# A two-layer decoder trunk on one core: token statistics moved behind their tile's matmuls, and two changes of PSUM bank

## The chip, the cores and the metric

The kernel runs on one core of one Trainium2 chip. The time is device time in microseconds (us) of one execution; the median of three executions is given. The profiled execution is one more, taken by the hardware profiler, with its own time and span. The engines are called as in the profile: PE (TensorE matmul), PEld (its weight load), DVE (VectorE), ACT (ScalarE), POOL (GpSimd), SP (SyncE, which issues the DMAs). "Granted clock" is the share of the full TensorE clock that was granted.

## The reference

All tensors are float32; 512 tokens, 1024 channels, two residual layers. Layer 0 has the gated and the attention mixer, layer 1 the matrix memory; each is followed by an MLP.

```python
def reference(x, ...):
    for layer in range(2):
        h = _rmsnorm(x, mix_norm_g[layer])
        x = x + (_even_mixer(h, ...) if layer % 2 == 0 else _odd_mixer(h, ...))
        h = _rmsnorm(x, mlp_norm_g[layer])
        x = x + jnp.square(jax.nn.relu(h @ mlp_w1[layer])) @ mlp_w2[layer]
    return x

def _rmsnorm(x, g):
    return x * lax.rsqrt(jnp.mean(x * x, -1, keepdims=True) + 1e-6) * g

def _even_mixer(h, ...):
    p = h @ w_in                                  # 1024 -> 2560
    za, zb = jax.nn.gelu(p[..., :1024]), p[..., 1024:]
    u, vg = za[..., :512], layernorm(za[..., 512:])   # groups of 64 columns
    y_a = u * (causal 128x128 mixing of vg per group + bias)
    q, k, v = zb in three parts; q and k RMS-normed per head of 64
    y_b = stick_breaking(q, k, v)                 # strictly causal attention, 8 heads
    return concat([y_a, y_b]) @ w_out

def _odd_mixer(h, ...):
    p = h @ w_in                                  # q, k, v, output gate, 8 gate columns
    hc = mlstm(silu(conv(q, k)), v, gates)        # 4 heads, chunks of 128
    return (rmsnorm(hc) * sigmoid(og)) @ w_out
```

## The kernel before

**Precision.** Every matrix product is made of three matmuls. An operand a is split into a high part (ACT copies it to the matmul type) and a low part (DVE subtracts the high part): a `hi`/`lo` pair. `mm3` (L289 to L292) issues high x high, high x low and low x high. Weights are read from HBM in units of 128 x 1024 (`w_load`), split by `w_split` (L189 on ACT, L190 on DVE, for a few units on POOL) and taken in order by `w_take`, which also starts the splitting of the next units. Raw units have two buffers there, split ones five.

**Norms.** The RMS norm is taken apart: the matmuls use x times the channel gain g, and the factor of the token, (mean square + eps)^-1/2, is applied to the product afterwards. For the first projection x comes in four tiles of 128 tokens. `x_load` brings a tile (or a half of it) in by DMA, multiplies it by g (L358, tile `xg`) and splits it into `xhi` and `xlo` (L286, L287). `x_stats` squares the tile on ACT (L363, `xq`, two buffers), adds the eight channel blocks on POOL in three steps (L365), and calls `norm_cols`: a matmul with a column of 1/1024 (L266, in a PSUM bank "C"), the addition of eps on DVE (L268), and a power on POOL (L270), which gives `r1[t]`; L368 keeps eps times the mean square in `er2[t]`. In the text `x_stats(0)` stands between the loads of tiles 2 and 3, the other three behind the last load, all of them ahead of the first chunk.

**The first projection.** `act_chunk` runs a chunk of 512 output columns over the four token tiles: 24 matmuls to a tile (8 channel blocks x 3) into one PSUM bank, then an evacuation. The chunks are vg, u, k, q and v. `vg_evac` (L407) applies Gelu with the factor `r1[t]` on ACT, then the layer norm of the row on DVE with a power on POOL (L415), and splits the result. The banks are called A (two), B (three), C (two) and O (one); the first chunks take A, A, O in turn.

**The MLP.** The hidden units are computed in four groups; the second product of a group is a 2 x 2 block product made of seven block products (`PROD`) instead of eight, in `second` (L658 to L714), each of 24 matmuls of 256 columns for each of two column halves s. `accm` collects what several groups share; in the last group (`done`) it is added to the residual `xs` and the finished rows are handed on (`yield d`) or shipped to HBM (`ship`). Before, product n1 is added to block (1, 1) of the residual from its bank "c", then n4 is accumulated on top of n1 in the same bank, and their sum is added to block (1, 0) in two halves (L709 to L714).

**Between blocks.** `enter` (L331 to L343) follows a generator that finishes the residual row by row: it scales and splits each row for the next layer (L282, L283), squares it (L335, L338) and adds up the squares (L339, on POOL, the last on DVE), and ends with `norm_cols`. `w_out` (L321 to L328) is an output projection: eight rows of channels, each in a PSUM bank named by `tags`, added to the residual by DVE (L327).

**Order.** Each engine works through its own queue in order. Which instruction stands where is settled before the run by a planner that lays the instructions out by simulated times, with earlier text ahead of later text among what is ready; semaphores follow from the tiles that are read and written. `tc.issue_after(ins)` makes the instructions traced in its block that run on the engine of `ins` stand behind `ins`.

## Time and profile before

| | |
|---|---|
| three executions | 1136.91, 1133.94, 1134.82 us, median 1134.82 |
| profiled execution | 1136.92 us, span 1135.1 us, granted clock 0.994 |
| PE busy | 1106.8 us, 98% of the span |
| PEld busy | 960.1 us, 85% |
| DVE busy | 828.4 us, 73% |
| ACT busy | 524.3 us, 46% |
| POOL busy | 161.9 us, 14% |
| DMA | 105.18 MB, mean 93 GB/s |

The span is the part of the execution in which the profiler saw the engines work. Busy time is the time in which an engine had at least one instruction running; matmuls overlap, so their durations add up to more. In rows of the profile "out<-in" are the tiles by the program's names; "[1.23 <-POOL xq L365]" behind a row says that the engine sat idle for 1.23 us before it and that POOL's instruction of line 365 on tile xq ended that.

### The profile page before, as it was taken

The numbers are of one execution on the slowest core, as the hardware profiler recorded it, in microseconds if no ns is written. First come the engines' busy times: TensorE is split into PE (matmuls) and PEld (weight loads), VectorE is DVE, ScalarE is ACT, GpSimd is POOL, SyncE is SP. The second block draws the span as 40 slices with busy tenths as digits, with TensorE's granted clock in tenths as the row PEclk, the third lists the DMA queues.
The fourth block names the chain that finished last, engine by engine and source line by source line (L and its number), as shares of the span: only waits on it lengthen the run. The fifth ranks groups of instructions, "written<-read, shape, count | busy, mean of one in ns | idle before, by whom it ended". The sixth has DMA issues, their size and how long they took to land.

```text
span 1135.1 us, 15928 instructions
## 1 busy us (share of the span) xinstructions
PE 1106.8 (98%) x6372; PEld 960.1 (85%) x6372; DVE 828.4 (73%) x1151; ACT 524.3 (46%) x800; POOL 161.9 (14%) x154
## 2 busy tenths in 40 slices
PE   8999979999999999999999999999999999999998
PEld 5788767878988988988988888887899899899898
DVE  7753599469957957957977676679887677677676
ACT  5343677445435435435555444435443444444442
POOL 7216554550000000000130010003100000000000
PEclk8999999999999999999999999999999999999999
DMA  6322310242241241341042203304324224224121
GB/s 230 93 75 79 104 41 1 74 168 93 94 132 72 96 138 65 100 143 56 20 132 76 94 19 112 94 31 155 112 74 141 82 74 147 76 75 149 38 84 66
DMA packets 34506, 105.18 MB, mean 93 GB/s; under 512 B 3712, under 2 KB 10112, under 8 KB 34432
## 3 DMA queue, kind: packets, MB, share of 16 engines
q1 hardware_dynamic: 34432, 104.17, 28.3%
q8 instruction: 50, 0.82, 0.3%
q14 instruction: 24, 0.20, 0.1%
HBM read 102.06 MB, written 2.10 MB: 92 GB/s over the span
## 4 chain that ended last, share of the span: by engine, by line
PE 82%; DVE 10%; POOL 3%; ACT 2%; issue 2%; DMA 1%; SPq 0%; DVEq 0%; ACTq 0%; POOLq 0%
PE psA L292 10%; PE psA L290 10%; PE psA L291 10%; PE psB L674 7%; PE psB L676 7%; PE psB L675 7%; PE psC L292 5%; PE psC L291 5%; PE psC L290 5%; DVE m L537 2%; PE psO L290 2%; PE psO L291 2%; PE psO L292 2%; DVE wl L190 2%; DMA wr<-wall 1%
## 5 line engine op out<-in xcount | busy, mean ns | idle before, releaser
L189 ACT ACTIVATE wh<-wr 128x1024 fp32r<-128x1024 f32 (+1 forms) x124 | 131.2, 1061 | 170.1 <-DMA wr<-wall 53.0
L190 DVE TENSOR_TENSOR wl<-wr,wh 128x1024 fp32r<-128x1024 f32 (+1 forms) x108 | 135.9, 1265 | 81.7 <-ACT wh L189 49.9
L189 ACT ACTIVATE wh<-wq_s 128x1024 fp32r<-128x1024 f32 x64 | 67.0, 1060 | 127.4 <-PE psC L291 56.3
L291 PE MATMUL psA<-xlo,wh 128*128 128x512 f32 x292 | 115.3, 395 | 0.0
L292 PE MATMUL psA<-xhi,wl 128*128 128x512 f32 x288 | 114.2, 396 | 0.5 <-DVE wl L190 0.5
L290 PE MATMUL psA<-xhi,wh 128*128 128x512 f32 x288 | 112.5, 392 | 1.1 <-DVE xres L327 1.1
L292 PE MATMUL psC<-xhi,wl 128*128 128x512 f32 x256 | 101.5, 396 | 0.0
L291 PE MATMUL psC<-xlo,wh 128*128 128x512 f32 x256 | 101.3, 396 | 0.0
L290 PE MATMUL psC<-xhi,wh 128*128 128x512 f32 x256 | 100.4, 392 | 0.0
L292 PE MATMUL psA<-wh,xlo 128*128 128x512 f32 (+2 forms) x232 | 88.1, 381 | 2.1 <-DVE xlo L287 1.8
L290 PE MATMUL psA<-wh,xhi 128*128 128x512 f32 (+2 forms) x232 | 88.7, 385 | 1.2 <-ACT wh L189 1.0
L291 PE MATMUL psA<-wl,xhi 128*128 128x512 f32 (+2 forms) x232 | 88.3, 382 | 1.1 <-DVE wl L190 1.1
L189 ACT ACTIVATE wh<-wq 128x1024 fp32r<-128x1024 f32 x48 | 50.8, 1058 | 79.0 <-PE psB L675 30.2
L339 POOL TENSOR_TENSOR ssq<-ssq,sq 128x512 f32<-128x512 f32 x18 | 31.6, 1753 | 346.7 <-ACT sq L338 346.7
L190 DVE TENSOR_TENSOR wl<-wq_s,wh 128x1024 fp32r<-128x1024 f32 x64 | 77.6, 1220 | 2.5 <-ACT wh L189 2.5
L290 PEld LDWEIGHTS psA<-xhi,wh 128*128 128x128 f32 x288 | 54.7, 190 | 13.8 <-ACT sq L338 1.5
L686 DVE TENSOR_TENSOR xres<-xres,psB 128x512 f32<-128x512 f32 (+1 forms) x96 | 54.7, 592 | 15.2 <-PE psB L676 15.1
L733 DVE SCALAR_TENSOR_TENSOR r<-psC,rrow 128x512 f32<-128x512 f32 x32 | 22.1, 690 | 59.6 <-PE psC L292 59.6
L291 PEld LDWEIGHTS psA<-xlo,wh 128*128 128x128 f32 x292 | 54.9, 188 | 12.3
L292 PEld LDWEIGHTS psA<-xhi,wl 128*128 128x128 f32 x288 | 54.1, 188 | 12.2 <-DVE wl L190 0.8
L190 DVE TENSOR_TENSOR wl<-wq,wh 128x1024 fp32r<-128x1024 f32 x48 | 58.6, 1221 | 2.2 <-ACT wh L189 2.2
L290 PEld LDWEIGHTS psC<-xhi,wh 128*128 128x128 f32 x256 | 48.6, 190 | 10.9
(396 smaller groups left out, 3146.6 us busy)
## 6 DMA issues: line engine op xcount, KB each, us to landing
wr<-wall SPq DMA_DIRECT2D x122, 512.0 KB, 3.5
wq<-wall SPq DMA_DIRECT2D x64, 512.0 KB, 3.6
out<-xres SPq DMA_DIRECT2D x16, 128.0 KB, 1.8
wr<-wv SPq DMA_DIRECT2D x2, 528.0 KB, 3.6
xres<-xT SPq DMA_DIRECT2D x4, 256.0 KB, 6.2
xres<-xT SPq DMA_DIRECT2D x2, 512.0 KB, 8.9
lngb<-lngb SPq DMA_DIRECT2D x1, 512.0 KB, 5.6
sgr<-sgw SPq DMA_DIRECT2D x1, 512.0 KB, 6.3
```

What stands on the lines that cost most here:

```text
L189: act.activation(hi[:, :n], raw, AF.Copy)
L190: (gp if i in POOL_LO else dve).tensor_tensor(lo[:, :n], raw, f(hi[:, :n]), op=ALU.subtract)
L290: pe.matmul(out, lhsT=lh, rhs=rh, start=first, stop=False)
L291: pe.matmul(out, lhsT=lh, rhs=rl, start=False, stop=False)
L292: pe.matmul(out, lhsT=ll, rhs=rh, start=False, stop=last)
L339: (dve if i == KT - 1 else gp).tensor_tensor(ssq, ssq, j, op=ALU.add)
L537: dve.tensor_tensor_scan(m[:, ::-1], m[:, ::-1], ones.to_broadcast([P, n]), 1.0, op0=ALU.mult, op1=ALU.mult)
L674: pe.matmul(o, lhsT=lh, rhs=rh, start=first, stop=False, skip_group_check=True)
L675: pe.matmul(o, lhsT=lh, rhs=rl, start=False, stop=False, skip_group_check=True)
L676: pe.matmul(o, lhsT=ll, rhs=rh, start=False, stop=fin, skip_group_check=True)
L686: add = lambda dst, b, op=ALU.add: dve.tensor_tensor(dst, dst, b, op=op)
L733: dve.scalar_tensor_tensor(r, b, 0.0, rb[0], op0=ALU.max, op1=ALU.mult)
```

## The change

Three edits. (1) `x_stats` is cut in two: `x_square` makes the squares and the adds, `x_stats` the matmul, eps, power and `er2`. `act_chunk` gets an argument `behind`, and calls it after the last matmul of each token tile, with the matmuls that it issues placed behind that one on TensorE; the vg chunk passes `x_stats`. The multiplication by g of tiles 1 to 3 is done by DVE instead of POOL, and the square of tile 0 is called before the loads of the other tiles. (2) In the last group of a layer n1's bank is closed with n1 alone; n1 is added to block (1, 1) and to block (1, 0), and n4 begins anew in a bank of the tag "C". (3) The odd layer's last output projection takes its banks in the order A, A, B, B instead of A, A, O.

```diff
@@ mm3
-        pe.matmul(out, lhsT=ll, rhs=rh, start=False, stop=last)
+        return pe.matmul(out, lhsT=ll, rhs=rh, start=False, stop=last)
@@ act_chunk
-    def act_chunk(hus, per, width, evac, tags=tags):
+    def act_chunk(hus, per, width, evac, tags=tags, behind=None):
...
-                mm3(b[:, :width], xhi[:, kt, tts(t)], xlo[:, kt, tts(t)], hi[:, o:o + width], lo[:, o:o + width],
-                    kt == 0, kt == KT - 1)
+                i = mm3(b[:, :width], xhi[:, kt, tts(t)], xlo[:, kt, tts(t)], hi[:, o:o + width], lo[:, o:o + width],
+                        kt == 0, kt == KT - 1)
+            if behind:
+                with tc.issue_after(i.ins):
+                    behind(t)
             evac(t, b[:, :width])
@@ first projection
-        def x_stats(t):
-            q = ld.tile([P, KT, P], F32, name=f"xq{t}", tag="xq", bufs=2)
+        xq = [None] * NT
+
+        def x_square(t):
+            q = xq[t] = ld.tile([P, KT, P], F32, name=f"xq{t}", tag="xq", bufs=2)
             act.activation(q, xs[:, :, tts(t)], AF.Square)
             for k in (4, 2, 1):
                 gp.tensor_tensor(q[:, :k], q[:, :k], q[:, k:2 * k], op=ALU.add)
-            me, r1[t] = norm_cols([q[:, 0, :]])
+
+        def x_stats(t):
+            me, r1[t] = norm_cols([xq[t][:, 0, :]])
             e = sm(1, "er2")
             dve.tensor_scalar(e, me, EPS, None, op0=ALU.mult)
             er2[t] = e
...
-        x_load(1, 0, 4, gp)
-        x_load(1, 4, 8, gp)
-        x_load(2, 0, 8, gp)
-        x_stats(0)
-        x_load(3, 0, 8, gp)
+        x_square(0)
+        x_load(1, 0, 4, dve)
+        x_load(1, 4, 8, dve)
+        x_load(2, 0, 8, dve)
+        x_load(3, 0, 8, dve)
         for t in range(1, NT):
-            x_stats(t)
+            x_square(t)
...
-        act_chunk(w_take(4), 2, 512, vg_evac)
+        act_chunk(w_take(4), 2, 512, vg_evac, behind=x_stats)
@@ mlp, second
-                    add(blk(1, 1, s), prod("n1", "c", True, False))
+                    b = prod("n1", "c", True, done)
+                    add(blk(1, 1, s), b)
                     ship(1, 1, s)
-                    b = prod("n4", "c", False, True)
+                    if done:
+                        add(blk(1, 0, s), b)
+                    b = prod("n4", "e" if done else "c", done, True, "C")
@@ odd layer
-        r = enter(w_out(w_take(2), y_of(3), "AAO"), 3, ssq)
+        r = enter(w_out(w_take(2), y_of(3), "AABB"), 3, ssq)
```

## The prediction

> **What bounds the kernel now.** I read the page first (shares of the engines), then the waits of TensorE, then the busy time by stretch, then the order of time at the four places that the diff touches. Times are us from the start of the span.

> ```profile
> PE 1106.8 (98%) x6372; PEld 960.1 (85%) x6372; DVE 828.4 (73%) x1151; ACT 524.3 (46%) x800; POOL 161.9 (14%) x154
> ```

> ```profile
> ...
> PE psB L674 <- DVE xres L686: 2.6, 2, 1.6
> ...
> PE psC L266 <- POOL xq L365: 2.1, 2, 1.2
> ```

> TensorE is the bound, 98% of the span. So time can come only out of its idle 28.3 (1135.1 - 1106.8) and out of matmuls that ran at a lower clock. The waits (columns: total, times, longest) name two causes that the diff touches; two single waits of the kind stand in the rows of parts 1 and 3.

> ```profile
> 0.00:46.00 46.00, 38.83 (x141) 28.00 (x142) 36.39 (x48) 22.82 (x27) 28.68 (x30) 0.89 0.55 179
> 8.00:34.00 26.00, 21.17 (x80) 16.53 (x81) 23.81 (x22) 12.88 (x15) 23.44 (x16) 0.86 0.60 195
> 100.00:250.00 150.00, 138.63 (x700) 110.75 (x699) 103.83 (x143) 89.14 (x171) 80.44 (x59) 0.99 0.21 64
> 562.00:585.00 23.00, 21.11 (x172) 20.50 (x170) 22.23 (x26) 12.91 (x18) 12.15 (x14) 1.00 0.39 115
> 780.00:802.00 22.00, 20.68 (x88) 15.63 (x86) 21.96 (x24) 13.70 (x20) 9.86 (x7) 1.00 0.57 191
> ```

> Columns: the stretch, its length, busy time of PE, PEld, DVE, ACT and POOL, granted clock, DMA share, GB/s. The first 46 us lose most: 7.2 idle and a clock of 0.89. Between 8 and 34 both DVE (23.81 of 26) and POOL (23.44) are nearly full. At 562 to 585 and 780 to 802 DVE has hardly a gap either: whatever TensorE saves there may be taken back by a vector operation that comes no earlier.

> **Part 1, the first projection.** The change takes the four gating multiplies from POOL to DVE, and the mean-square matmuls from where the planner had put them to just behind the 24 products of their token tile. Squares, adds, matmuls and powers stay in number, and the DMAs keep their order on SP's queue.

> ```profile
> 8.93 0.50 PE L291 MATMUL psA<-wl,xhi 128*128 128x512 f32 x1 [1.06 <-DVE wl L190]
> ...
> 10.33 0.63 PE L292 MATMUL psA<-wh,xlo 128*128 128x512 f32 x1
> 10.75 0.63 PE L290 MATMUL psA<-wh,xhi 128*128 128x512 f32 x1
> 12.61 0.59 PE L266 MATMUL psC<-onesd,xq 128*128 128x1 f32 x2 [1.23 <-POOL xq L365]
> 13.06 0.77 PE L291 MATMUL psA<-wl,xhi 128*128 128x512 f32 x1
> ...
> 29.14 0.40 PE L291 MATMUL psO<-wl,xhi 128*128 128x512 f32 x1
> 29.37 0.39 PE L292 MATMUL psO<-wh,xlo 128*128 128x512 f32 x1
> 29.61 0.28 PE L266 MATMUL psC<-onesd,xq 128*128 128x1 f32 x2
> 30.72 0.38 PE L266 MATMUL psC<-onesd,xq 128*128 128x1 f32 x2 [0.84 <-POOL xq L365]
> 30.96 0.48 PE L290 MATMUL psA<-wh,xhi 128*128 128x512 f32 x1
> 31.28 0.40 PE L291 MATMUL psA<-wl,xhi 128*128 128x512 f32 x1
> ...
> 33.51 0.79 PE L292 MATMUL psA<-wh,xlo 128*128 128x512 f32 x1 [1.83 <-DVE xlo L287]
> ...
> 36.97 0.40 PE L291 MATMUL psA<-wl,xhi 128*128 128x512 f32 x1
> ```

> That was TensorE's order of time (start, duration, line, operation, what ended the idle time before). DVE's, and then its groups between 8 and 34 (count, busy time, mean ns, idle before):

> ```profile
> 3.99 0.69 DVE L358 TENSOR_TENSOR xg<-xres,par 128x512 f32<-128x512 f32 x1 [2.28 <-DMA xres<-xT]
> ...
> 10.49 3.14 DVE L190 TENSOR_TENSOR wl<-wr,wh 128x1024 fp32r<-128x1024 f32 x2
> ```

> ```profile
> L190 DVE TENSOR_TENSOR wl<-wr,wh 128x1024 fp32r<-128x1024 f32 x5 | 9.1, 1830 | 0.0
> L287 DVE TENSOR_TENSOR xlo<-xg,xhi 128x512 fp32r<-128x512 f32 x3 | 3.5, 1180 | 1.6 <-ACT xhi L286 1.6
> L287 DVE TENSOR_TENSOR xlo<-xg,xhi 128x1024 fp32r<-128x1024 f32 x2 | 3.5, 1769 | 0.0
> ```

> The same weight split between 300 and 500, and POOL's groups of the first 50 us:

> ```profile
> L190 DVE TENSOR_TENSOR wl<-wr,wh 128x1024 fp32r<-128x1024 f32 x22 | 26.6, 1221 | 16.6 <-PE psB L676 15.8 <-ACT wh L189 0.8
> ```

> ```profile
> L365 POOL TENSOR_TENSOR xq<-xq 128x512 f32<-128x512 f32 (+2 forms) x12 | 13.6, 1143 | 7.6 <-ACT xq L363 7.3
> L358 POOL TENSOR_TENSOR xg<-xres,par 128x512 f32<-128x512 f32 (+1 forms) x4 | 8.4, 2088 | 0.0
> L270 POOL TENSOR_TENSOR rc<-me,nhalf 128x1 f32<-128x1 f32 x4 | 3.5, 890 | 4.9 <-DVE me L268 4.9
> ```

> A product at full speed takes 0.23 from start to start (29.14 to 29.37). Four terms:

> (a) Tile 0. The product of 13.06 stood behind the statistics, which waited for POOL's adds. It needs the first of the two weight splits that began at 10.49 and took 3.14 together, so that one ended near 12.06. TensorE can resume at 12.1: 0.95 gained.

> (b) The statistics of tiles 1 and 2 kept the products from 29.61 to 30.96, and the next start came 0.32 later instead of 0.23: 1.44 in all. A pair alone costs 0.24 (30.72 to 30.96) and that 0.09, so 0.33, and three pairs now stand between the tiles, 1.0 (tile 0's was counted in (a), tile 3's was paid before too). Gain 0.45.

> (c) Tile 3 waited for its low part from 31.51 (31.28 + 0.23) to 33.51: 2.0. The multiply ahead of that split was POOL's last. POOL loses 8.4; DVE gains two multiplies of 0.69 and two of twice the size, taken at twice that, 4.1. Is the low part then in time? From 12.06 DVE owes two weight splits (3.7), the multiplies (4.1) and four splits of x (2 x 1.18 + 2 x 1.77 = 5.9), at the crowded prices of now: 25.8. Tile 3 wants it near 30. Even 4 us of other work put ahead would not delay it.

> (d) After that wait eight starts, 33.51 to 36.97, took 3.46 instead of 8 x 0.23 = 1.84: 1.6 lost at the lower clock, gone with the wait. Here idling for about 2 us was enough to lower it. [...] The trace shows the loss, so I count it.

> Part 1: 0.95 + 0.45 + 2.0 + 1.6 = 5.0. The norm factor now comes about 1.5 after its tile (pair, DVE, a power of 0.89 on POOL), and the evacuation on ACT waits for it; behind it wait the next weight splits on ACT, not yet wanted, and its PSUM bank, wanted two tiles of 24 x 0.23 = 5.5 later. POOL's adds are 12 x 1.14 / 4 = 3.4 a tile. The squares have two buffers, so tile 2's waits for tile 0's pair, near 18 (tile 2 ended at 29.6, two tiles earlier is 18.5, less (a)); square and adds end near 23, wanted near 29. The next weight units are released by TensorE's own progress and move with it.

> **Part 2, the last product of a layer.** In the last group n4 gets a bank of its own, and n1 is added to two blocks instead of being summed with n4 first.

> ```profile
> 1127.02 1.29 DVE L686 TENSOR_TENSOR xres<-xres,psB 128x512 f32<-128x512 f32 x2 [3.89 <-PE psB L676]
> ...
> 1127.17 0.28 PE L676 MATMUL psB<-n1h,wl 128*128 128x256 f32 x1
> ...
> 1128.45 0.36 PE L674 MATMUL psB<-n4h,wh 128*128 128x256 f32 x1 [1.00 <-DVE xres L686]
> ```

> ```profile
> 572.89 0.28 PE L292 MATMUL psO<-wh,xlo 128*128 128x264 f32 x1
> 574.80 0.39 PE L674 MATMUL psB<-n4h,wh 128*128 128x256 f32 x1 [1.63 <-DVE xres L686]
> ...
> 584.39 0.51 PE L292 MATMUL psA<-wh,xlo 128*128 128x264 f32 x2 [0.26 <-DVE xlo L283]
> ```

> These matmuls start 0.12 apart (half the columns of 0.23). At the end of the kernel n4 could start at 1127.29 instead of 1128.45: 1.15. The added DVE add (0.65, half of 1.29) ends near 1129.0, n4 near 1130.2, so it is covered, and only the final adds and the output follow, which move along. In the first layer the same wait is worth up to 574.80 - 573.01 = 1.8, but there DVE is busy 22.23 of 23, gets two adds more (1.3), and already ends the stage: TensorE waits for low parts of x at 584.39. Bounds -1.3 and 1.8; nearest to a full DVE, I take 0.3.

> **Part 3, banks AABB** for the odd layer's last output projection: the following MLP's first bank no longer waits for the last adds.

> ```profile
> 788.68 0.39 PE L292 MATMUL psA<-yoh,wl 128*128 128x512 f32 x1
> 790.18 0.47 PE L290 MATMUL psA<-xhi,wh 128*128 128x512 f32 x1 [1.11 <-DVE xres L327]
> ...
> 795.09 2.44 DVE L283 SCALAR_TENSOR_TENSOR xlo<-xres,par,xhi 128x512 fp32r<-128x512 f32 x2
> ```

> TensorE could go on at 788.91 instead of 790.18: 1.3. But the last low parts come at 797.5 from a DVE busy 21.96 of 22, and without them the first MLP product cannot end. Bounds 0 and 1.3; I take 0.5.

> **Sum:** 5.0 + 1.15 + 0.3 + 0.5 = 6.95. The profiled execution took 1136.92 (its span and 1.8 around it), so 1130.0 for it. It lay 2.1 above the median of the three runs, 1134.82, from which I forecast **1127.9**. The three lie 3.0 apart, so some 0.3%, 3.4 us, is what can be told from no change.

> **Rivals.**

> *The clock recovers in tile 0.* If the shorter pause before the product of 13.06 (0.9 instead of 1.9) lets the clock rise at once, some eight starts take 0.23 instead of 0.42 (10.33 to 10.75): 1.5 more, 1126.4. Against it: the pause of 1.06 before 8.93 was followed by starts at the lower clock. [...] Chance 0.12.

> *DVE becomes the bound of the start.* It gets 4.1 more where 2.2 are free. For it: a weight split takes 1.83 beside a busy POOL and 1.22 later. Against it: POOL's work falls by 8.4 of 23.4. If masks, gate weights and evacuations are put ahead, tile 3 still waits and tile 1 waits by another 1 us: of part 1 only (a) and (b) less 1 are left, 0.4, with the rest 2.35: 1132.5. [...] Chance 0.17.

> *The norm factor comes late.* If the power for tile 0 is queued on POOL behind the adds of tiles 2 and 3, it ends near 30, and the bank that tile 3 wants near 29.6 is free near 30.8: 1.2 idle and 1.6 of clock, 1130.7. Chance 0.05.

> *The planner lays out attention otherwise.* The order on the engines follows simulated times, which shift. TensorE idles 11.4 between 100 and 250 (150 - 138.6); half as much again is 5.7: 1133.6. Chance 0.08.

> *Slower: TensorE stalls behind each tile.* The pairs stand in order in its queue, so where a tile's adds are late, the next tile's products wait too. [...] It decides from adds that end over 6 us later than I reckon. Chance 0.08.

> **How the numbers follow.** The forecast has 0.50, with a range of its own from 1125.6 (upper bounds of parts 2 and 3) to 1130.0 (lower ones). The range of all, 1123.8 to 1133.0, adds both of the clock's gain below and the DVE case above; it leaves out the slow case, most of attention's and a tail of either side, 0.18. Faster than 1131.4: 0.50 + 0.12 + 0.05, and a quarter of the DVE case, 0.71. Slower than 1138.2: 0.08. Same: 0.21.

> **What would show it.** Right: in the first 40 us no wait of L292 for xlo and none of L266 for xq; each L266 pair behind 24 products; a clock above 0.93 over the first 46; POOL without L358; n4 in psC at the end, 0.12 behind n1. Near 573 and 790 the waits gone, but a new one of about 1 us for xlo L283 near 583 and 796. Wrong: TensorE waiting in tile 1 or 3 for xlo, L266 waiting for L365 behind a tile, L407 late enough that a product waits for its bank, or an idle sum between 100 and 250 far from 11.4.

## The result, and the profile after

The change made the kernel slower: 1141.92 us (median of six, 1140.51 to 1143.23) against 1135.59 (six, 1133.56 to 1137.73), ratio 1.0056 [1.0045, 1.0066]. The forecast was 1127.9. The profiled execution took 1140.83, span 1139.1, 4.0 more than before.

First the page's line of TensorE, then its list of waits (total, times, longest), both of the changed kernel.

```profile
PE 1108.0 (97%) x6372; PEld 962.1 (84%) x6372; DVE 831.1 (73%) x1159; ACT 522.9 (46%) x800; POOL 155.2 (14%) x150
```

```profile
PE psC L266 <- DVE ssq L343: 5.3, 2, 3.9
...
PE psA L290 <- ACT sq L342: 2.5, 1, 2.5
PE psA L290 <- ACT xhi L282: 2.2, 1, 2.2
...
PE psA L292 <- DVE xlo L283: 1.5, 1, 1.5
...
PE psA L291 <- DVE xlo L283: 1.1, 1, 1.1
```

The two kinds of wait named in the prediction, n4 for the residual and L266 for xq, are gone. New ones stand in their place, at the end of the first layer and where the odd layer's last output projection hands over to its MLP (called the end of the odd layer here). The largest is the mean-square matmul at that second place (L266), which waits 3.95 for the last sum of squares. Four of the stretches shown before, in the changed kernel (columns as there):

```profile
0.00:46.00 46.00, 41.36 (x164) 29.86 (x165) 39.11 (x56) 24.07 (x29) 23.36 (x26) 0.96 0.56 183
100.00:250.00 150.00, 140.03 (x703) 111.90 (x702) 101.88 (x142) 89.28 (x171) 79.99 (x58) 0.98 0.23 75
562.00:585.00 23.00, 19.37 (x147) 18.96 (x146) 19.83 (x25) 7.94 (x11) 7.75 (x14) 0.93 0.37 118
780.00:802.00 22.00, 17.14 (x72) 12.94 (x70) 21.93 (x22) 13.38 (x20) 10.81 (x7) 1.00 0.57 191
```

The start got better as forecast: 41.36 busy instead of 38.83, clock 0.96 instead of 0.89. Between 100 and 250 TensorE idles 10.0, and 11.4 before, so nothing was lost in the attention. At 562 to 585 and 780 to 802 TensorE lost 1.7 and 3.5 of busy time, though these windows hold somewhat later work than before, because the kernel is 3 to 6 us ahead there.

To see where a kernel gains or loses, I add up the columns of all matmuls in order of time and ask when each kernel reaches the same sum. The table gives that time minus the time before, at eight points of the kernel before (negative: ahead), with the medians and ratios of all kernels run. Each group was run beside the kernel before on the same chip. The eight columns come from one profiled execution of each kernel; differences in the text are taken before rounding.

| kernel | median us | ratio [95%] | 40 | 560 | 577 | 590 | 780 | 793 | 806 | end |
|---|---|---|---|---|---|---|---|---|---|---|
| changed kernel | 1141.92 | 1.0056 [1.0045, 1.0066] | -5.2 | -5.7 | -7.4 | -2.9 | -3.0 | -2.1 | 5.7 | 4.0 |
| p1_alone | 1132.03 | 0.9969 [0.9958, 0.998] | -4.5 | -4.4 | -4.4 | -4.0 | -3.9 | -4.0 | -4.0 | -4.0 |
| p2_alone | 1137.15 | 1.0011 [1.0, 1.0022] | -1.1 | -1.3 | -3.0 | 0.9 | 1.0 | 1.0 | 1.1 | -0.6 |
| p3_alone | 1145.78 | 1.0084 [1.0069, 1.0099] | 0.1 | 0.3 | 0.3 | 0.7 | 0.9 | 3.3 | 8.4 | 8.5 |
| p1_and_p2 | 1132.47 | 0.9971 [0.9962, 0.998] | -4.2 | -5.7 | -7.4 | -1.9 | -2.0 | -2.1 | -2.0 | -3.7 |
| order_only | 1142.68 | 1.0063 [1.0043, 1.0083] | -2.7 | -2.8 | -2.8 | -2.2 | -2.2 | -2.2 | 3.9 | 3.9 |
| square_first | 1135.76 | 1.0005 [0.9994, 1.0016] | -5.3 | -5.7 | -7.3 | -1.9 | -2.0 | 0.3 | 0.9 | -0.8 |
| rows_in_order | 1137.18 | 1.0013 [1.0004, 1.0022] | -4.6 | -0.4 | -2.1 | 3.8 | 3.6 | 1.7 | 3.0 | 1.1 |
| rows_in_order_odd | 1131.29 | 0.9955 [0.9942, 0.9969] | -4.5 | -3.8 | -5.5 | -1.7 | -1.8 | -3.7 | -3.2 | -4.9 |
| n4_last_only | 1130.24 | 0.9955 [0.994, 0.997] | -5.2 | -5.4 | -5.4 | -5.5 | -5.5 | -5.5 | -5.5 | -7.1 |
| n4_no_second_add | 1129.75 | 0.9953 [0.9937, 0.9969] | -4.7 | -6.6 | -7.0 | -5.4 | -5.3 | -5.3 | -5.3 | -7.2 |
| multiplies_only | 1131.94 | 0.9968 [0.9957, 0.9979] | -4.4 | -6.0 | -6.0 | -6.2 | -6.0 | -6.0 | -6.0 | -6.0 |
| statistics_only | 1132.02 | 0.9965 [0.9952, 0.9977] | -4.9 | -6.5 | -6.5 | -6.7 | -6.8 | -6.8 | -6.8 | -6.8 |
| statistics_and_n4_last | 1129.82 | 0.9948 [0.9935, 0.996] | -5.4 | -5.2 | -5.2 | -5.4 | -5.4 | -5.4 | -5.5 | -7.0 |
| all_mended | 1128.68 | 0.9941 [0.9928, 0.9953] | -4.9 | -6.4 | -6.4 | -6.5 | -6.5 | -8.4 | -7.7 | -9.3 |

Row one tells the story: 5.2 ahead after the start, 2.8 lost at the end of the first layer (560 to 590), 8.6 lost at the end of the odd layer (780 to 806), 1.7 regained after it, 1.2 of them in the last ten us. TensorE in the changed kernel at the first place, then at the second:

```profile
572.60 0.39 PE L290 MATMUL psA<-wh,xhi 128*128 128x264 f32 x1 [2.17 <-ACT xhi L282]
...
575.05 0.59 PE L292 MATMUL psA<-wh,xlo 128*128 128x264 f32 x1 [1.46 <-DVE xlo L283]
575.44 0.42 PE L290 MATMUL psA<-wh,xhi 128*128 128x264 f32 x1
575.66 0.42 PE L291 MATMUL psA<-wl,xhi 128*128 128x264 f32 x1
```

```profile
788.12 0.47 PE L290 MATMUL psA<-xhi,wh 128*128 128x512 f32 x1 [2.48 <-ACT sq L342]
...
804.70 1.86 PE L266 MATMUL psC<-onesd,ssq 128*128 128x1 f32 x8 [3.95 <-DVE ssq L343]
...
807.00 0.63 PE L291 MATMUL psC<-xlo,wh 128*128 128x512 f32 x1
```

In both places a pause is followed by matmuls at half speed: 0.22 from start to start at 575.44 where the narrow products take 0.12, and a wide one lasts 0.63 at 807.00 where 0.39 is usual.

At the very end n4 follows n1 without a pause, as forecast:

```profile
1132.64 0.28 PE L684 MATMUL psB<-n1h,wl 128*128 128x256 f32 x1
1132.76 0.28 PE L684 MATMUL psC<-n4h,wl 128*128 128x256 f32 x1
```

### The profile page after: what moved, and what is told of

Read it like the earlier page. It is cut to its first block, busy times and chain, and to the rows that moved or that the text cites. A ratio compares the mean times of both kernels' runs of the same rounds, so it can differ in the third digit from the quotient of the medians.

```text
span 1139.1 us, 15930 instructions
## 1 busy us (share of the span) xinstructions
PE 1108.0 (97%) x6372; PEld 962.1 (84%) x6372; DVE 831.1 (73%) x1159; ACT 522.9 (46%) x800; POOL 155.2 (14%) x150
## 4 chain that ended last, share of the span: by engine, by line
PE 85%; DVE 10%; issue 2%; ACT 2%; DMA 1%; POOL 1%; DVEq 0%; SPq 0%; ACTq 0%; POOLq 0%
PE psA L292 11%; PE psA L291 11%; PE psA L290 11%; PE psB L682 7%; PE psB L684 7%; PE psB L683 7%; PE psC L292 5%; PE psC L291 5%; PE psC L290 5%; PE psO L290 2%; DVE m L545 2%; PE psO L292 2%; PE psO L291 2%; DVE wl L190 2%; PE psO L684 1%
## 5 line engine op out<-in xcount | busy, mean ns | idle before, releaser
L189 ACT ACTIVATE wh<-wr 128x1024 fp32r<-128x1024 f32 (+1 forms) x124 | 131.3, 1061 | 182.2 <-DMA wr<-wall 57.2
L190 DVE TENSOR_TENSOR wl<-wr,wh 128x1024 fp32r<-128x1024 f32 (+1 forms) x108 | 135.4, 1259 | 83.1 <-ACT wh L189 51.3
L189 ACT ACTIVATE wh<-wq_s 128x1024 fp32r<-128x1024 f32 x64 | 67.1, 1060 | 130.9 <-PE psC L291 57.8
L291 PE MATMUL psA<-xlo,wh 128*128 128x512 f32 x292 | 115.3, 395 | 1.1 <-DVE xlo L283 1.1
L290 PE MATMUL psA<-xhi,wh 128*128 128x512 f32 x288 | 112.6, 392 | 2.5 <-ACT sq L342 2.5
L292 PE MATMUL psA<-xhi,wl 128*128 128x512 f32 x288 | 114.0, 396 | 0.4 <-DVE wl L190 0.4
L292 PE MATMUL psC<-xhi,wl 128*128 128x512 f32 x256 | 102.9, 402 | 0.0
L291 PE MATMUL psC<-xlo,wh 128*128 128x512 f32 x256 | 102.5, 401 | 0.0
L290 PE MATMUL psC<-xhi,wh 128*128 128x512 f32 x256 | 101.9, 398 | 0.0
L290 PE MATMUL psA<-wh,xhi 128*128 128x512 f32 (+2 forms) x232 | 88.5, 384 | 3.4 <-ACT xhi L282 2.2
L292 PE MATMUL psA<-wh,xlo 128*128 128x512 f32 (+2 forms) x232 | 87.8, 379 | 2.2 <-DVE xlo L283 1.5
L291 PE MATMUL psA<-wl,xhi 128*128 128x512 f32 (+2 forms) x232 | 88.1, 381 | 1.6 <-DVE wl L190 1.5
L189 ACT ACTIVATE wh<-wq 128x1024 fp32r<-128x1024 f32 x48 | 50.8, 1058 | 78.1 <-PE psB L683 28.1
L190 DVE TENSOR_TENSOR wl<-wq_s,wh 128x1024 fp32r<-128x1024 f32 x64 | 77.7, 1222 | 2.5 <-ACT wh L189 2.5
L343 POOL TENSOR_TENSOR ssq<-ssq,sq 128x512 f32<-128x512 f32 x18 | 29.3, 1627 | 352.4 <-ACT sq L342 352.4
L290 PEld LDWEIGHTS psA<-xhi,wh 128*128 128x128 f32 x288 | 54.6, 190 | 15.1 <-ACT sq L342 2.9
L291 PEld LDWEIGHTS psA<-xlo,wh 128*128 128x128 f32 x292 | 54.9, 188 | 13.6 <-DVE xlo L283 1.6
L292 PEld LDWEIGHTS psA<-xhi,wl 128*128 128x128 f32 x288 | 54.1, 188 | 12.1 <-DVE wl L190 0.8
L190 DVE TENSOR_TENSOR wl<-wq,wh 128x1024 fp32r<-128x1024 f32 x48 | 59.3, 1235 | 2.3 <-ACT wh L189 2.3
L290 PEld LDWEIGHTS psC<-xhi,wh 128*128 128x128 f32 x256 | 49.5, 193 | 11.2
```

The lines of the kernel that those rows point to most:

```text
L189: act.activation(hi[:, :n], raw, AF.Copy)
L190: (gp if i in POOL_LO else dve).tensor_tensor(lo[:, :n], raw, f(hi[:, :n]), op=ALU.subtract)
L290: pe.matmul(out, lhsT=lh, rhs=rh, start=first, stop=False)
L291: pe.matmul(out, lhsT=lh, rhs=rl, start=False, stop=False)
L292: return pe.matmul(out, lhsT=ll, rhs=rh, start=False, stop=last)
L343: (dve if i == KT - 1 else gp).tensor_tensor(ssq, ssq, j, op=ALU.add)
```

## The experiments

**Which part does it?** Each part alone, and the first two together, against the kernel before. (In p2_alone and p3_alone `x_stats` is cut in two as well, but both halves are called in the old places.)

```diff
# p1_alone: edit (1) of the change; p2_alone: edit (2); p1_and_p2: both
# p3_alone: edit (3)
-        r = enter(w_out(w_take(2), y_of(3), "AAO"), 3, ssq)
+        r = enter(w_out(w_take(2), y_of(3), "AABB"), 3, ssq)
```

> Part 1 alone (statistics behind their tiles, multiplies on DVE); parts 2 and 3 as in the kernel before. Theory A (the loss comes from the planner's new order at the end of the odd layer, which part 3 makes, and from part 2 in the first layer): about 6 us faster than before, ratio 0.995, tile 3 of the first chunk ending 5.3 us earlier and the lead kept to the end. Theory B (the loss comes from part 1: a shifted start makes the planner lay out everything later in another way): 0 to 2 us slower.

> Part 2 alone, in both layers. Theory A: the first layer loses about 2.6 us (TensorE runs ahead of DVE, pauses for xhi and xlo and falls to the lower clock), the last gains 1.2: 1 to 1.5 us slower, ratio 1.001. Theory B: both waits go and nothing comes for them, 1.5 us faster.

> Part 3 alone (banks AABB). Theory A: the last square of the odd layer stands on ACT behind two weight splits and its addition on DVE behind two more, the statistics come 3 to 4 us late, then TensorE runs at the lower clock: 8 us slower, ratio 1.007. Theory B: within 1 us of before.

> Parts 1 and 2 without part 3. Theory A: the sum of the two alone, 4 to 5 us faster than before, ratio 0.996, and 10 to 11 us faster than the changed kernel. Theory B: 0 to 1 us slower than before.

Part 1 gains (0.9969, less than the 0.995 expected), part 2 is worth nothing by itself (1.0011) and nothing on top of part 1 (0.9971), part 3 costs 0.84%. So the whole slowdown comes with one string of bank letters. p3_alone shows the two waits of the changed kernel by itself:

```profile
PE psC L266 <- DVE ssq L343: 5.1, 2, 3.6
...
PE psA L290 <- ACT sq L342: 2.5, 1, 2.5
```

**Why do bank letters cost 8 us?** The order on ACT and DVE answers. Around 800 in the kernel before, ACT, DVE and TensorE:

```profile
798.72 0.64 ACT L338 ACTIVATE sq<-xres 128x512 f32<-128x512 f32 x1 [1.74 <-POOL ssq L339]
800.24 2.21 ACT L189 ACTIVATE wh<-wr 128x1024 fp32r<-128x1024 f32 x2 [0.89 <-PE psA L291]
```

```profile
800.94 0.68 DVE L339 TENSOR_TENSOR ssq<-ssq,sq 128x512 f32<-128x512 f32 x1
```

```profile
801.68 1.05 PE L266 MATMUL psC<-onesd,ssq 128*128 128x1 f32 x8
```

And in the changed kernel:

```profile
798.74 1.06 ACT L189 ACTIVATE wh<-wr 128x1024 fp32r<-128x1024 f32 x1 [0.89 <-PE psA L291]
800.56 1.06 ACT L189 ACTIVATE wh<-wr 128x1024 fp32r<-128x1024 f32 x1 [0.76 <-PE psA L291]
801.53 0.61 ACT L342 ACTIVATE sq<-xres 128x512 f32<-128x512 f32 x1
```

```profile
801.69 2.35 DVE L190 TENSOR_TENSOR wl<-wr,wh 128x1024 fp32r<-128x1024 f32 x2
803.96 0.68 DVE L343 TENSOR_TENSOR ssq<-ssq,sq 128x512 f32<-128x512 f32 x1
```

Before, the last square is done at 799.36, ahead of two weight splits on ACT. In the changed kernel the planner put it behind them: 802.14. Its addition on DVE moved behind two `wl` splits. Those weights are for later; they only wait for TensorE to release their buffers, and the square, which the end of the block needs, waits in the same queue. I took that for the cause, and the new banks themselves for the rival. Two kernels tell them apart: the kernel before with the bad order forced upon it, and the changed kernel with the good order forced upon it.

```diff
# order_only: the kernel before, banks AAO; whi lists the weights' splits on ACT;
# w_take(2, 7) in the odd layer's last w_out, so that the unit exists
-                act.activation(j, xs[:, d, :], AF.Square)
+                with tc.issue_after(whi[wpos[0] + 6 if norm == 3 and i == KT - 1 else 0].ins):
+                    act.activation(j, xs[:, d, :], AF.Square)
# square_first: the changed kernel; two weight units start behind the last square
-                act.activation(j, xs[:, d, :], AF.Square)
+                sq = act.activation(j, xs[:, d, :], AF.Square)
+                if norm == 3 and i == KT - 1:
+                    with tc.issue_after(sq.ins):
+                        next(units)
+                        next(units)
# and w_take(2, LAV) in that w_out, two units fewer ahead
```

> The kernel before, banks AAO, but the last square of the odd layer made to stand on ACT behind the two weight splits behind which part 3 alone had put it (one more unit is split ahead for that). Theory A (the place of that square is what part 3 costs): statistics 3 us or more late, 5 to 9 us slower than before. Theory C (the banks themselves, through the waits of the first MLP product for DVE, cost it): within 1.5 us of before.

> The changed kernel with all three parts, banks AABB, but the last two weight units split ahead of the MLP are traced behind the odd layer's last square, so that this square and its addition go first. Theory A: the wait of the statistics for the sum falls from 3.9 to under 1 us, 7 to 10 us faster than the changed kernel, near 1133. Theory C: no more than 2 us faster than the changed kernel.

order_only lost 6.1 between 780 and 806 with the old banks, by the same wait:

```profile
802.98 1.86 PE L267 MATMUL psC<-onesd,ssq 128*128 128x1 f32 x8 [3.62 <-DVE ssq L341]
```

In square_first the wait shrank from 3.95 to 0.81, and the loss of that stretch from 8.6 to 2.9. So the order of that square, with its addition, costs 5.7 of 8.6; the ratios of the two kernels, 1.0056 and 1.0005, say 5.8. What is left sits at 780 to 793 (TensorE of square_first):

```profile
789.08 0.77 PE L290 MATMUL psA<-xhi,wh 128*128 128x512 f32 x1 [2.48 <-DVE xres L331]
789.64 0.63 PE L291 MATMUL psA<-xlo,wh 128*128 128x512 f32 x1
...
802.55 1.05 PE L266 MATMUL psC<-onesd,ssq 128*128 128x1 f32 x8 [0.81 <-DVE ssq L347]
```

**Why does the MLP's first bank still wait, and longer than before (2.48 against 1.11)?** The additions of the last rows on DVE, in the changed kernel:

```profile
784.35 0.69 DVE L331 TENSOR_TENSOR xres<-psB,xres 128x512 f32<-128x512 f32 x1
...
787.29 0.68 DVE L331 TENSOR_TENSOR xres<-psA,xres 128x512 f32<-128x512 f32 x1
...
788.55 0.68 DVE L331 TENSOR_TENSOR xres<-psA,xres 128x512 f32<-128x512 f32 x1
```

The rows are written A, A, B, B, A, A, B, B, so that the last two should leave the banks A to the MLP. The planner plays them B, B, B, A, A, B, A, A: the last two are in A again. The addition of 787.29 ends at 787.97, and the product of 788.12 starts 0.15 later, as in square_first (788.93 and 789.08). The "ACT sq" of the wait's label is only what ended last by the profile. To see it, the rows are held in the order as written. The first attempt took in the attention mixer's projection as well, which also uses A, A, B, B, and lost 4.2 there by 560; the second holds the odd layer's rows alone.

```diff
# rows_in_order: square_first, and in w_out
+        i = None
...
+              with tc.issue_after(i.ins) if i and tags == "AABB" else ExitStack():
-                mm3(b, hi[:, tts(d)], ...)
+                i = mm3(b, hi[:, tts(d)], ...)
# rows_in_order_odd: the condition also asks for len(hus) == 2
```

> square_first, with one thing more: the eight rows of the odd layer's last output projection keep on TensorE the order in which they are written (banks A, A, B, B, A, A, B, B), each behind the one before. In the changed kernel and in square_first the planner plays them as B, B, B, A, A, B, A, A, so that the last two additions free banks of tag A, which the MLP's first product is waiting for. Theory (the order of the rows, not the number of banks, leaves the 2.48 us wait of L290 near 788): the wait shrinks under 0.5 us, the 2.3 us lost between 780 and 793 shrink to 0.5 or less, the time is 1 to 2.5 us below square_first, near 1133.5, ratio 0.998 to 0.9995. Rival 1 (DVE's low parts of x bound this stretch whatever the banks are): the MLP's first matmuls start earlier but L291 or L292 waits for xlo as long, the stretch of 780 to 806 loses the same 3 us within 0.7, 1135 to 1136. Rival 2 (the fixed order makes the projection wait for a bank of tag A in its middle): a wait there of 1 us or more and a time above square_first.

> rows_in_order pinned the rows of the attention mixer's projection too, which also takes the banks A, A, B, B, and lost 5 us there between 190 and 245; here only the odd layer's last projection keeps its written row order, the rest is square_first. Theory (the order of the rows leaves the wait): the first MLP product starts right behind the last row, the stretch of 780 to 806 costs 1.3 to 2 us less than in square_first, the time is 1133.5 to 1134.7, ratio 0.998 to 0.9995. Rival 1 (DVE bounds the stretch whatever the rows' order): what the first product gains is lost at the mean square, time within 0.7 us of square_first (1135.76). Rival 2 (the loss in the attention came from elsewhere and not from the pinned rows): a loss of 3 us or more between 190 and 245 again.

TensorE and then DVE of rows_in_order_odd:

```profile
786.32 0.39 PE L292 MATMUL psB<-yoh,wl 128*128 128x512 f32 x1
786.54 0.39 PE L290 MATMUL psA<-xhi,wh 128*128 128x512 f32 x1
```

```profile
785.23 0.68 DVE L332 TENSOR_TENSOR xres<-psA,xres 128x512 f32<-128x512 f32 x1
...
787.11 0.68 DVE L332 TENSOR_TENSOR xres<-psB,xres 128x512 f32<-128x512 f32 x1
...
788.37 0.68 DVE L332 TENSOR_TENSOR xres<-psB,xres 128x512 f32<-128x512 f32 x1
```

The MLP's first product now starts right behind the last row, while its additions are still to come, and the stretch of 780 to 806 gains 1.4 where square_first lost 2.9. The time fell from 1135.76 to 1131.29, twice what I had expected. rows_in_order, with the same rows at this place, gains 0.6 in the stretch.

**Why does part 2 gain nothing?** The lead falls by 2.1 to 4.2 at 560 to 590 wherever n4 has its own bank in the first layer and n1 is added twice. Either TensorE only runs ahead of DVE and waits there, or the two additions given to DVE cost the time.

```diff
# n4_last_only: parts 1 and 2, the second in the last layer alone
+                    own = done and last
-                    b = prod("n1", "c", True, done)
+                    b = prod("n1", "c", True, own)
# (and `own` for `done` in the two places below)
# n4_no_second_add: parts 1 and 2; the first layer's n1 is not added to block (1, 0)
-                    if done:
+                    if done and last:
                         add(blk(1, 0, s), b)
```

> Parts 1 and 2 without part 3, part 2 in the last layer alone. Theory A: as parts 1 and 2 without the loss of 2.6 us in the first layer: 5 to 6 us faster than before, ratio 0.995, some 2 us faster than parts 1 and 2 together. Rival (the first layer's loss is the planner's chance and not due to part 2): equal to parts 1 and 2, 0.997.

> Parts 1 and 2 without part 3, where the first layer's n1 is not added to block (1, 0) (left out of the computation), so that n4 has its own bank and DVE no additional work. If the two added additions on DVE cost the first layer its time: the loss there goes, 5 to 6 us faster than before. If it is TensorE's running ahead (n4 done early, then pauses for xhi and xlo and the lower clock): as parts 1 and 2, 3 to 4 us faster than before, with the pauses near 570 and 574 still there.

The first leaves the sum of n1 and n4 as it was in layer 0, the second leaves an addition out. Without the additions the loss at 560 to 590 falls from 3.9 (p1_and_p2) to 1.2; with n1 and n4 in one bank there is none (-5.4 to -5.5). The waits of p1_and_p2, then of n4_no_second_add:

```profile
PE psA L290 <- ACT xhi L282: 2.1, 1, 2.1
PE psA L292 <- DVE xlo L283: 2.0, 1, 2.0
```

```profile
PE psA L292 <- DVE xlo L283: 1.2, 1, 1.2
```

So both are true, and the additions cost more: 2.7 by this pair. The pair is one execution against one. The six executions that have both additions lose 2.1 to 4.2, which is 0.9 to 3.0 more than n4_no_second_add, and the ratios of the pair (0.9971 and 0.9953) say 2.0. The spread goes with the granted clock between 560 and 590: 0.94 in the changed kernel, which loses 2.8, and 0.89 in square_first, which loses 3.8 (1.00 before). The 1.2 that stays without the additions is TensorE running ahead: pauses of 0.35, 0.54, 1.25 and 0.87, 3.0 in all, stand where the kernel before has 1.63 (n4's bank), 0.26 and 0.21, 2.1 in all; that is 0.9 of the 1.2. n4_last_only was faster than both kernels.

**Do the four terms of part 1 stand by themselves?** One edit of it each: the multiplies on DVE with the statistics where they were, and the statistics behind the tiles with the multiplies on POOL.

```diff
# multiplies_only
-        x_load(1, 0, 4, gp)
+        x_load(1, 0, 4, dve)
# (the same for the other three)
# statistics_only: edit (1), but
+        x_load(1, 0, 4, gp)
# (the same for the other three)
```

> The kernel before with one edit of part 1: DVE instead of POOL multiplies tiles 1 to 3 by the channel gain; the mean-square matmuls stay where the planner puts them. Theory (my terms stand as separate causes): the wait of TensorE for tile 3's low part goes, with the slow matmuls behind it, terms (c) and (d), 3.6 us, at equal TensorE work by 40 us; the waits of L266 for xq stay or shrink, since POOL's adds come sooner; ratio about 0.997. Rival 1 (the terms hang together: the freed POOL also brings the adds early, so the matmuls need not be moved at all): the whole lead of part 1, 4.3 to 5 us, ratio 0.9955 to 0.9965. Rival 2 (without the matmuls moved behind the tiles, the planner puts them ahead of a tile's products and they wait): under 2 us.

> The kernel before with the other edit of part 1: the mean-square matmuls stand behind the 24 products of their token tile and the square of tile 0 comes ahead of the other loads; the multiplies of tiles 1 to 3 stay on POOL. Theory (separate terms): terms (a) and (b), 1.4 us at equal TensorE work by 40 us, and the wait for tile 3's low part stays near 1.8 us with slow matmuls behind it; ratio 0.998 to 0.9995. Rival 1 (hang together): POOL, which now has four multiplies and twelve adds, brings the adds too late for a place behind the tile, so that L266 or the next tile waits there: no lead at 40 us, or a loss of 1 to 3 us. Rival 2: the matmuls' place makes the whole lead, 4 us or more.

They do not: each edit alone gives the whole of part 1 (0.9968 and 0.9965 beside 0.9969 for both). In multiplies_only tile 3 does not wait for its low part. In statistics_only POOL still multiplies, and yet tile 3 does not wait either (tile 2 does, for 0.83). DVE of statistics_only, where the split of the last tile starts at 25.09, and of the kernel before, where it starts at 31.14:

```profile
25.09 2.31 DVE L287 TENSOR_TENSOR xlo<-xg,xhi 128x1024 fp32r<-128x1024 f32 x1
27.32 0.68 DVE L417 BATCH_NORM_STATS2 bs<-vge 128x6 f32<-128x512 f32 x1
```

```profile
30.27 0.94 DVE L417 TENSOR_TENSOR vge<-vge,lngb 128x512 f32<-128x512 f32 x1
31.14 2.31 DVE L287 TENSOR_TENSOR xlo<-xg,xhi 128x1024 fp32r<-128x1024 f32 x1
```

Before, tile 0's statistics came early, so its evacuation and layer norm were ready early, and the planner put them ahead of the last tile's split. With the statistics behind the tile, the layer norm comes later and the split stands ahead of it. POOL's multiply was not what held it: in the kernel before that had ended at 26.47 and ACT's high part at 27.56, and until 31.14 the split stood behind other work on DVE.

**The pieces together.** First the cheaper form of part 1 with n4's bank in the last layer; then all three parts, each as the runs had mended it.

```diff
# statistics_and_n4_last: n4_last_only with x_load(..., gp) as before
# all_mended: rows_in_order_odd with `own = done and last` as in n4_last_only
```

> n4_last_only with the multiplies of tiles 1 to 3 back on POOL: the statistics behind the tiles, and n4 in a bank of its own in the last layer only. Theory (the two edits of part 1 remove the same waits, and part 2 is worth 1.2 us at the very end whatever the start does): lead over before -4.9 at 40 us and 1.2 us more at the end, ratio 0.9945 to 0.996, within 1 us of n4_last_only (1130.24). Rival (the multiplies' engine still counts once the rest is changed): 1.5 us or more above n4_last_only, ratio 0.997 or more.

> All three parts with what the runs showed put right: part 1 whole, n4's own bank in the last layer only, banks A, A, B, B with the rows in written order and the weight units behind the last square. If the effects add: lead over before 5.2 us at 40, nothing lost at the first layer's end, -0.6 to +0.6 us in the stretch of 780 to 806, 1.2 us at the end; 1129.3 to 1130.8, ratio 0.9945 to 0.996, no more than 1 us beside n4_last_only. Rival (the mended part 3 is worth its 1.3 us or more by itself): under 1129, ratio below 0.9945. Rival (part 3 still loses): 1131.5 or more.

Both beat the kernel before and the changed one. In all_mended the stretch of 780 to 806 gains 1.2, the end another 1.6: 1128.68, 0.59% below before and 13.2 below the changed kernel. Against n4_last_only (1130.24) the intervals overlap, so that the mended part 3 adds something is shown by the traces (-5.5 to -5.5 there, -6.5 to -7.7 here), less surely by the times.

## Why the prediction was wrong

**Part 1 was right in direction and near in size.** 5.0 was forecast; the nine profiled kernels with the whole part are 4.2 to 5.3 ahead at 40 us, 4.8 in the mean. Some of this is the chance of the one execution I worked from: three kernels with the old start stand at -2.7, -1.1 and 0.1, with that execution itself -0.9 in the mean. In order_only and p2_alone tile 3 waits only 0.73, and the clock stays full in the first (1.00 between 20 and 46) and drops in the second (0.93); in p3_alone it waits 1.81, and the next products start 0.43 apart (0.87 between 20 and 46). Against that mean part 1 is worth 3.9, and the ratio of p1_alone, 0.9969, says 3.5. Terms (c) and (d) were thus taken from an execution that had the full wait. The rows of the changed kernel show the steps:

```profile
11.77 0.50 PE L291 MATMUL psA<-wl,xhi 128*128 128x512 f32 x1 [0.42 <-DVE wl L190]
12.11 0.40 PE L292 MATMUL psA<-wh,xlo 128*128 128x512 f32 x1
...
16.16 0.28 PE L266 MATMUL psC<-onesd,xq 128*128 128x1 f32 x2
...
17.74 0.50 PE L292 MATMUL psA<-wh,xlo 128*128 128x512 f32 x1 [0.74 <-DVE xlo L287]
```

(a) holds: the product that stood at 13.06 starts at 11.77 (12.39 in p1_alone; 12.1 was forecast). (b) holds: the pair stands behind the tile and costs nothing but itself. (c) holds in its effect, not in its cause: I put it down to POOL's last multiply. Moving the multiplies does remove the wait, but so does statistics_only with the multiplies still there; what held the split was its place in DVE's queue. The rival of DVE as bound of the start did not come; one wait of 0.74 in tile 1 is all. The rival of the clock came true in this execution (0.23 from start to start from 12.11 on, clock 0.91 over the first 20 us) and not in p1_alone (0.83), so I take it for chance rather than an effect of the edit.

**Part 2 was right at the end of the kernel and mis-sized in the first layer.** At the end 1.15 was forecast; after 1126 every kernel that has it gains 1.2. In the first layer I took +0.3 from bounds of -1.3 and 1.8, and it was -2.8 in the changed kernel, outside the bounds. The term that was too small is the lower bound: I charged the two additions with their own 1.3. They also pushed back the last low parts and the last sum of squares on a full DVE (18.68 busy of 19.20 between 562.0 and 581.2 in p1_and_p2; the last ssq addition starts at 581.19 in p1_and_p2, at 578.96 in n4_last_only), and the pauses that this made, 2.17 and 1.46 in the changed kernel, were followed by the lower clock of 575.44 (0.22 from start to start). I had counted that very price in term (d) of part 1 and not here. The forecast wait of about 1 us for xlo L283 near 583 came as 1.46 at 575.

**Part 3 is the step that failed.** "Bounds 0 and 1.3; I take 0.5", and it lost 8.6. The bounds took for granted that the instructions of ACT, DVE and TensorE keep their order, and asked only when a bank comes free. But an order settled by a planner is an output of the edit. Two reorderings, neither of them needed, cost 5.7 (the last square behind two weight splits) and 4.3 (the rows, which put the A banks last again); with both undone, the same banks gain 0.6, 1.4 and 1.2 in the three kernels that have it so, and the upper bound was 1.3. The wait for xlo that was forecast near 796 came (1.14 at 795.43), but the wait at 790 did not go: it grew to 2.48. Why the planner laid these two out otherwise, no run shows. The rival in which the planner lays out attention otherwise named the mechanism, at another place and for 5.7 us; I gave it 0.08 and did not ask it of the place that the diff touched. The rival on the slower side, TensorE stalling behind each tile, did not happen.

## What to carry to other kernels

Where a planner sets the order, a change of a buffer or a bank is also a change of order, and a bound worked out with the old order is no bound: ask which instruction at the end of the stage could be put behind work that is not yet wanted, and pin that one. When an edit frees a resource, read in the trace whether its users still come in the order that was meant. Two edits that both end the same wait are not worth their sum, and an execution that happens to show a wait in full overstates what removing it brings.

## What was new of the hardware

Pauses of about the same length were followed by a lower clock or were not. After 1.74 us idle, statistics_only ran on at 0.23 from start to start, its whole first 20 us at clock 1.00; after 1.83 the kernel before ran at 0.43 (33.51), and after 2.48 square_first slowed too (0.63 long at 789.64) while the changed kernel did not (its matmuls behind 788.12 stand 0.23 apart). Windows and rows of statistics_only:

```profile
0.00:20.00 20.00, 14.92 (x51) 8.65 (x52) 14.84 (x16) 11.13 (x13) 12.51 (x14) 1.00 0.94 305
```

```profile
12.18 0.50 PE L291 MATMUL psA<-wl,xhi 128*128 128x512 f32 x1 [1.74 <-DVE wl L190]
12.52 0.40 PE L292 MATMUL psA<-wh,xlo 128*128 128x512 f32 x1
12.75 0.39 PE L290 MATMUL psA<-wh,xhi 128*128 128x512 f32 x1
```

```profile
786.53:789.95 3.42, 1.83 (x8) 1.57 (x9) 3.42 (x5) 2.88 (x6) 2.80 (x3) 1.00 0.96 316
```

In square_first most of the 2.48 lay in one step, with TensorE busy for 1.28, and the next step ran at half clock:

```profile
785.32:788.74 3.42, 1.28 (x6) 0.71 (x4) 3.42 (x5) 2.88 (x5) 2.65 (x3) 1.00 0.31 47
788.74:792.15 3.41, 3.08 (x7) 2.47 (x8) 3.41 (x5) 1.79 (x3) 1.16 (x1) 0.50 1.01 414
```

In these two traces, between the first few us and the last matmul, seven steps at full clock had TensorE idle for 2.02 to 2.85 (from 6.10, 29.99 and 149.46 on before; from 4.88, 134.59, 571.49 and 800.19 on in the changed kernel), and one at half clock followed each. None at full clock there had between 1.63 and 2.02. The one of 1.63 (572.71, before) was followed by full clock, and so were the shorter ones, but for one of 1.19 (236.99, changed kernel). What decided there stays open.

A price for such a pause, in this kernel, is the pause and, where a step at half clock follows, some 1.6 more (term (d) of the prediction, a wait followed by one step: from 33.51 on eight starts took 3.46 instead of 1.84 before the change).
